# One DRAM record for each step of the RWKV recurrence, and exponents copied through DRAM

## The chip, the core and the metric

The kernel is one program on one NeuronCore of a Trainium2 chip. Its five engines have a queue each and run it in the order written: TensorE (PE in the profile, its weight loads PEld), VectorE (DVE), ScalarE (ACT), GpSimd (POOL) and SyncE (SP, which here only issues DMA transfers). The metric is the device time of one execution in microseconds.

## The reference

One layer of a hybrid block over a context of 256 tokens and 1024 latent tokens, width 1024. The normed and modulated input goes through one projection `h @ w_in` that feeds three groups; their outputs are joined and projected back; then a mixture of experts follows. The group that the change touches most is RWKV-7, four heads of 64, run forward and backward:

```python
def step(s, inp):
    r_t, w_t, k_t, v_t, a_t, b_t = inp
    sa = jnp.einsum('bhvk,bhk->bhv', s, a_t)
    s = s * w_t[:, :, None, :] + sa[..., None] * b_t[:, :, None, :] + v_t[..., None] * k_t[:, :, None, :]
    return s, jnp.einsum('bhvk,bhk->bhv', s, r_t)
```

The second group is a state space model (Mamba-2, chunks of 128), whose exponents are differences of a running sum: `decay_in = exp(where(causal, a_cs[..., :, None] - a_cs[..., None, :], -inf))`. The third is gated linear attention (GLA, chunks of 64), which carries a state of 32 by 64 a head from chunk to chunk.

## The kernel before, in words

RWKV is computed in chunks of 64 tokens, 20 of them for the 1280 tokens. Work on a chunk has three parts.

*Segments* (`rw_seg`, line 401). A segment is 256 tokens of one pair of heads (block b = 0 or 1); with five segments and two directions d a block has ten segment-directions. Each gives, per chunk: AR (decayed -kk and r), BK (b and k, decayed the other way), G (the 128x128 products of BK and AR under a mask: `psg`, line 463, and line 465), and BT, a transpose of BK (`ptb`, line 478). v is transposed as well (`ptv`, line 419). All this is stored to DRAM from SP: `vtD` (v), `mabD` (the half of G for the same head: MA in columns 0 to 63 and MB in 64 to 127), and `stepD` (AR, the other half of G, and BT, in 1536 columns for each chunk). That is 11 stores for a segment-direction. Tiles AR, BK, G have two buffers, BT one.

*Inverses* (`rw_inverse`, line 511). MA is read from `mabD` and a triangular inverse is built from it in 32x32 pieces (`px`); it goes to `sD`. There are three calls, the first 4 chunks of both blocks last (`i1`).

*Recurrence* (`rw_step`, line 599, 20 steps). `rw_loads` (line 576) reads the step's operands: `cd` from `stepD` (768 KB), half of `sm` from `sD`, from step 4 on the other half from `mabD` (MB, two loads), and `v` from `vtD` (two loads): six loads. Then a chain on TensorE, ScalarE and VectorE: pa from v and the state Z, copied to rh; pb from S and rh, copied to u; pz from v and u, added into the next Z. `py` is the output (latent chunks only).

Between these, TensorE does the big projection of the input (`psi`, lines 261 to 263): weights come in tiles of 512 KB (`wraw`, line 250, three buffers, loaded by SP too), are split into a high and a low part (whi, wlo), and multiply the 1280 tokens in pieces of 512 and 256 columns. Where the recurrence runs, the work of the other groups stands between its steps: GLA's states (`gla_states`, ptk and pkv), the exponents of the state space model (`ssd_dt`) and its states. `ssd_dt` puts the three bf16 parts of the running sums (`parts`, tile csp) into `difD`, from which `df` is read later; it takes 48 small stores (lines 1056 to 1058).

The order in each queue is set at build time by the framework's scheduler, from dependencies, buffers and its own estimates of durations. So a change of tiles and transfers can move instructions far from the lines that the diff touches.

Of the kernel before, what the change touches and what calls it, by code (L numbers as in the profile page):

```python
# [16 lines left out]
F = mybir.dt.float32  # L17
# [3 lines left out]
AF = mybir.ActivationFunctionType  # L21
# [9 lines left out]
TT = TC + TL  # L31
# [283 lines left out]
HS = [slice(0, 64), slice(64, 128)]  # L315
# [10 lines left out]
def rw_consts(g):  # L326
    nc, P = g.nc, g.ab
# [15 lines left out]

    g.stepD = g.dram.tile([128, 20, 1536], F, name="stepD")

    g.mabD = g.dram.tile([2, 128, 20, 2, 128], F, name="mabD")
    g.sD = g.dram.tile([2, 128, 20, 128], F, name="sD")
    g.vtD = g.dram.tile([20, 64, 512], F, name="vtD")
    g.bvD = g.dram.tile([2, 128, TL], F, name="bvD")
# [51 lines left out]
def rw_seg(g, b, s, r, k, v, wa, kk):  # L401

    nc = g.nc
    t0, n, pos = SEGS[s]
    T = lambda tag, bufs=2, w=256: g.tmp.tile([128, w], F, tag=tag, name=tag, bufs=bufs)
    ts = slice(t0, t0 + n)
    r, k, v, wa, kk = r[:, ts], k[:, ts], v[:, ts], wa[:, ts], kk[:, ts]
    nch = n // 64
    for d in range(2):
        p0, bd = pos[d], 2 * b + d  # L410
        pp = slice(p0, p0 + nch)
        if d:
            vd = T("sq")[:, 0:n]
            nc.scalar.activation(vd[:, ::-1], v, AF.Copy)
        else:
            vd = v
        pt = g.ps.tile([128, 4, 128], F, tag="tp", name="ptv")
        for i in range(n // 128):
            nc.tensor.transpose(pt[:, i, :], vd[:, 128 * i:128 * i + 128], g.ident)
        vt = T("vt", 2, 258)[:, 0:n].rearrange("p (i c) -> p i c", c=128)  # L420
        nc.scalar.activation(vt, pt[:, 0:n // 128], AF.Copy)
        nc.sync.dma_start(g.vtD[pp, :, 128 * bd:128 * bd + 128].rearrange("(i q) t c -> (q t) i c", q=2), vt)
        ps = g.ps.tile([128, 2, 256], F, tag="tp", name="psl")
# [35 lines left out]
        G = T("G", 2, 1024).rearrange("p (c h t) -> p c h t", h=2, t=128)[:, 0:nch]  # L459
# [6 lines left out]
        for h in range(2):  # L466
            o, u = HS[h], HS[1 - h]
            x0 = 384 * bd
            nc.sync.dma_start(g.mabD[b, o, pp, d], G[o, :, h, :])
            nc.sync.dma_start(g.stepD[o, pp, x0:x0 + 128], arf[o])  # L470
            nc.sync.dma_start(g.stepD[o, pp, x0 + 128:x0 + 256], G[u, :, h, :])
# [3 lines left out]
        for c0 in range(0, nch, 4):  # L475
            pt = g.ps.tile([128, 4, 128], F, tag="gm", name="ptb")
# [99 lines left out]
def rw_loads(g, p):  # L576

    nc, T = g.nc, g.rw
    cd = T.tile([128, 1536], F, tag="cd", name="cd", bufs=2)
    nc.sync.dma_start(cd, g.stepD[:, p])  # L580
    sm = T.tile([128, 2, 4, 64], F, tag="sm", name="sm", bufs=2)
    nc.sync.dma_start(sm[:, 0].rearrange("p (b q) t -> p b (q t)", b=2), g.sD[:, :, p].rearrange("b s t -> s b t"))
    if p >= 4:
        for b in range(2):
            nc.sync.dma_start(sm[:, 1, 2 * b:2 * b + 2], g.mabD[b, :, p, :, 64:128])
    v = T.tile([128, 4, 64], F, tag="v", name="v", bufs=3)
    for h in range(2):
        nc.sync.dma_start(v[HS[h]], g.vtD[p].rearrange("t (q h c) -> t q h c", q=4, h=2)[:, :, h, :])
    return cd.rearrange("p (q k t) -> p k q t", q=4, k=6), sm, v

# [8 lines left out]
def rw_step(g, p):  # L599
# [3 lines left out]
    at = lambda t: lambda q, h: t[h, q]  # L603
    cd, sm, v = rw_loads(g, p)
    a, r, ak, rk, bb, bk = (cd[:, k] for k in range(6))
    S, MB = sm[:, 0], sm[:, 1]
    ps = lambda tag, name: g.ps.tile([128, 4, 64], F, tag=tag, name=name)
# [43 lines left out]
def rw_finish(g):  # L651
    nc = g.nc
    for b in range(2):
        for t0 in (0, 512):
            ts = slice(t0, t0 + 512)
            x = g.rw.tile([128, 1536], F, tag="cd", name="fw", bufs=2)
            yc, bv, gt = (x[:, 512 * i:512 * i + 512] for i in range(3))
            sq = g.rw.tile([128, 512], F, tag="sm", name="fs", bufs=2)
            nc.sync.dma_start(bv, g.bvD[b, :, ts])
# [129 lines left out]
def gla_states(g):  # L789

    nc = g.nc
    W = g.gl
    glT = W.tile([16, TT], F, name="glT")
    for tl in range(10):
# [4 lines left out]
    g.gq = [W.tile([128, 3, TL], F, name=f"gq{d}") for d in range(2)]  # L799
    g.gS = W.tile([128, 2, 20, 64], F, name="gS")  # L800
    sc = 32 ** -0.5
# [10 lines left out]
    for d in range(2):  # L812
        nc.scalar.activation(la[:, d], la[:, d], AF.Ln, bias=g.epsc[:, 3:4])
        nc.gpsimd.tensor_sub(la[:, d], g.gq[d].rearrange("p i t -> p (i t)")[:, 0:TT], la[:, d])
    for d in range(2):
        rv = (lambda x: x[:, ::-1]) if d else (lambda x: x)
# [164 lines left out]
def ssd_dt(g):  # L981
# [64 lines left out]
    for i in range(3):  # L1046
        nc.vector.tensor_copy(parts[:, 0:2, i], cs)
        if i < 2:
            nc.vector.tensor_sub(cs, cs, parts[:, 0:2, i])
    nc.vector.tensor_scalar(parts[:, 2], parts[:, 0], -1.0, None, op0=OP.mult)  # L1050
    for d in range(2):
        for q in range(2):
            for h in range(4):
                src = parts[64 * d + 4 * q + h:64 * d + 64:8]
                o = 64 * q + 3 * h
                nc.sync.dma_start(g.difD[:, o + 12 * d:o + 12 * d + 3, h], src[:, 0])
                nc.sync.dma_start(g.difD[:, o + 24:o + 27, 4 + d], src[:, 2])
                nc.sync.dma_start(g.difD[:, o + 24:o + 27, 6 + d], src[:, 1])

# [807 lines left out]
```

## Time and profile before

| | us |
|---|---|
| median of 3 runs | 1532.99 |
| lowest, highest | 1532.07, 1540.90 |
| profiled execution | 1533.99 |
| its span | 1532.2 |
| TensorE busy | 1340.5 (87%) |
| VectorE busy | 785.2 (51%) |
| mean granted TensorE clock | 0.89 of full |

The stages follow one another: norm and first projections to about 120 us, segments of block 0 and 1 to about 411 us, convolution and inverses to about 556 us (both with projections between them), the recurrence to about 738 us, outputs of the state space model and GLA to about 905 us, then output projection and experts. A window row gives busy time of each engine, so the fullest engine of a stretch can be seen; a timeline row gives one run of like instructions with the wait ahead of it in brackets; the table of waits says what a tile's instruction waited for. An SP row is the time to issue a transfer, not to land it.

### The profile page before, as it was taken

The page shows a single profiled execution, that of the slowest core. Times are in us where ns is not written, and L with a number is a line of the kernel's source. Part 1 is how long each engine was busy: PE and PEld are TensorE (multiplying, and loading weights), DVE is VectorE, ACT ScalarE, POOL GpSimd, SP SyncE. Part 2 cuts the span into 40 slices and gives each one's busy share as a digit, 9 for nine tenths or more (in the row PEclk, how much of TensorE's full clock was granted, in tenths as well). Part 3 has the DMA queues.
Part 4 walks back from the last instruction along what each step waited for, and adds up shares of the span by engine and source line. Part 5 has one row for each costly group of instructions (what it writes and reads, how often), then busy time and mean ns, then how long its engine had stood idle before and what let it go on. Part 6 is the DMA issues. An engine that isn't in the chain of part 4 may idle for free. (4 is left out here: it accounts for less than half of the span.)

```text
span 1532.2 us, 28018 instructions
## 1 busy us (share of the span) xinstructions
PE 1340.5 (87%) x11077; PEld 1111.9 (73%) x11077; DVE 785.2 (51%) x1482; ACT 515.4 (34%) x1056; POOL 389.5 (25%) x432
## 2 busy tenths in 40 slices
PE   7897899999797776777889989993999999999984
PEld 3585677777676774666557767762999999999984
DVE  4849868889979854414564472227102212112532
ACT  5544334443363134422433352220212212212333
POOL 3312432343334111413453252112101111111112
PEclk9997899999899777889856589995999999999998
DMA  9454867677661467476544365425988868868984
GB/s 320 134 156 138 201 153 169 167 189 180 162 144 31 93 141 203 127 229 207 185 145 118 97 208 171 145 97 193 368 299 288 271 201 301 294 224 299 311 266 123
DMA packets 297253, 296.81 MB, mean 194 GB/s; under 512 B 114281, under 2 KB 214890, under 8 KB 297119
## 3 DMA queue, kind: packets, MB, share of 16 engines
q1 hardware_dynamic: 288095, 269.81, 57.7%
q0 software_dynamic: 7872, 20.97, 5.7%
q10 hardware_dynamic: 1152, 4.19, 0.7%
q8 instruction: 89, 1.46, 0.4%
q14 instruction: 45, 0.37, 0.1%
HBM read 221.44 MB, written 73.72 MB: 193 GB/s over the span
## 5 line engine op out<-in xcount | busy, mean ns | idle before, releaser
L1576 PE MATMUL p<-hT,w 128*128 128x144 f32 (+10 forms) x2048 | 263.2, 288 | 0.0
L1576 PEld LDWEIGHTS p<-hT,w 128*128 128x128 f32 x2048 | 257.6, 192 | 0.6
L262 PE MATMUL psi<-hlo,whi 128*128 128x512 f32 (+1 forms) x440 | 172.0, 391 | 5.0 <-DVE hlo L234 3.8
L261 PE MATMUL psi<-hhi,whi 128*128 128x512 f32 (+1 forms) x440 | 170.3, 389 | 0.0
L263 PE MATMUL psi<-hhi,wlo 128*128 128x512 f32 (+1 forms) x440 | 169.9, 387 | 0.3 <-POOL wlo L254 0.3
L1583 PE MATMUL p<-hid,w 128*128 128x144 f32 (+10 forms) x1024 | 136.6, 294 | 8.4 <-DVE hid L1578 7.2
L1583 PEld LDWEIGHTS p<-hid,w 128*128 128x128 f32 x1024 | 133.9, 199 | 9.0 <-DVE hid L1578 7.5
L1602 POOL DMA_INDIRECT acc<-yr,rows x27 | 41.4, 1532 | 323.0 <-DVE yr L1598 188.2
L1578 DVE TENSOR_TENSOR hid<-hid,p 128x144 f32<-128x144 f32 (+10 forms) x64 | 18.7, 294 | 170.0 <-PE p L1576 165.9
L262 PEld LDWEIGHTS psi<-hlo,whi 128*128 128x128 f32 x440 | 85.6, 195 | 26.0 <-DVE hlo L234 5.6
L263 PEld LDWEIGHTS psi<-hhi,wlo 128*128 128x128 f32 x440 | 85.4, 194 | 19.1 <-issue 3.4
L261 PEld LDWEIGHTS psi<-hhi,whi 128*128 128x128 f32 x440 | 85.8, 195 | 17.7 <-issue 2.1
L1598 DVE TENSOR_SCALAR yr<-pty,rows 128x512 f32<-128x512 f32 (+8 forms) x46 | 32.7, 741 | 112.4 <-PE pty L1592 105.2
L1584 ACT ACTIVATE yT<-p,mods 128x144 f32<-128x144 f32 (+10 forms) x128 | 43.0, 374 | 112.7 <-PE p L1583 112.5
L1577 ACT ACTIVATE hid<-p 128x144 f32<-128x144 f32 (+10 forms) x64 | 18.2, 284 | 168.8 <-PE p L1576 168.7
L739 DVE SCALAR_TENSOR_TENSOR co<-gr,pc,co 128x512 f32<-128x512 f32 x72 | 59.4, 849 | 6.5 <-ACT co L728 4.7
L190 DVE SCALAR_TENSOR_TENSOR aacc<-wada,csig,aacc 128x512 f32<-128x512 f32 x56 | 51.6, 921 | 15.6 <-DMA wada<-in_ada_w_dram 15.3
L262 PE MATMUL pso<-wol,mh 128*128 128x512 f32 x128 | 52.8, 412 | 3.3 <-DVE wol L1222 2.2
L261 PE MATMUL pso<-woh,mh 128*128 128x512 f32 x128 | 52.4, 412 | 1.0 <-DVE go L1265 1.0
L263 PE MATMUL pso<-woh,ml 128*128 128x512 f32 x128 | 52.6, 411 | 0.0
L463 PE MATMUL psg<-AR,BK 64*128 64x128 f32 x320 | 46.6, 304 | 4.0 <-DVE BK L456 1.6
L463 PEld LDWEIGHTS psg<-AR,BK 64*128 64x128 f32 x320 | 39.5, 204 | 13.4 <-issue 4.0
(540 smaller groups left out, 2668.3 us busy)
## 6 DMA issues: line engine op xcount, KB each, us to landing
w<-in_moe_w_dram SPq DMA_DIRECT2D x47, 2048.0 KB
wada<-in_ada_w_dram SPq DMA_DIRECT2D x32, 512.0 KB
cd<-stepD SPq DMA_DIRECT2D x20, 768.0 KB
wraw<-in_w_in_dram SPq DMA_DIRECT2D x24, 512.0 KB
aw<-in_ada_w_dram SPq DMA_DIRECT2D x10, 512.0 KB
stepD<-AR SPq DMA_DIRECT2D x40, 128.0 KB
mabD<-G SPq DMA_DIRECT2D x40, 128.0 KB
stepD<-G SPq DMA_DIRECT2D x40, 128.0 KB
```

What stands on the lines that cost most here:

```text
L190: nc.vector.scalar_tensor_tensor(acc, w[:, k % 2], g.sg[:, k, 0:1], acc, op0=OP.mult, op1=OP.add)
L261: nc.tensor.matmul(ps, whi(k), xhi(k), start=k == 0, stop=False)
L262: nc.tensor.matmul(ps, whi(k), xlo(k), start=False, stop=False)
L263: nc.tensor.matmul(ps, wlo(k), xhi(k), start=False, stop=k == 7)
L463: nc.tensor.matmul(pg[h][:, c, :], bkf[HS[h], c], arf[HS[h], c], start=True, stop=True)
L739: nc.vector.scalar_tensor_tensor(o, src(dy, dx), w(3 * dy + dx), o, op0=OP.mult, op1=OP.add)
L1576: nc.tensor.matmul(p[:, 0:n], w[:, k, fs], hT[:, k, s0:s0 + n], start=k == 0, stop=k == 7)
L1578: nc.vector.tensor_mul(hid[:, f, 0:n], hid[:, f, 0:n], p3[:, 0:n])
L1583: nc.tensor.matmul(p[:, 0:n], w2[:, f, 128 * k:128 * k + 128], hid[:, f, 0:n], start=f == 0, stop=f == 3)
L1584: nc.scalar.activation(yT[:, k, 0:n], p[:, 0:n], AF.Copy, scale=g.mods[:, 40 + k, 0:1])
L1598: nc.vector.tensor_scalar(yr[0:m, h], pf, wt[0:m, b:b + 1], None, op0=OP.mult)
L1602: nc.gpsimd.indirect_dma_start(out=g.acc, out_offset=bass.IndirectOffsetOnAxis(ap=rows[0:m, 0, b:b + 1], axis=0), in_=yr[0:m, :], in_offse ...
```

## The change

- `stepD` grows from 1536 to 2048 columns: MB (columns 64 to 127 of G's half) and v go into it. `vtD` is dropped and `mabD` holds MA alone. In a segment, each of the two stores of G to `mabD` becomes two stores of half the width, and v is transposed in 64x64 blocks, so that it lies by head as the record wants it. A segment-direction has 13 stores instead of 11; 80 of G's stores are 64 KB with 256-byte pieces.
- A step of the recurrence loads `rec` (1024 KB) and `S` (128 KB), each with three buffers, where it had six loads and two buffers (three for v). Steps 0 to 3 now load MB as well, which they don't use.
- `difD` is filled from a DRAM copy of the parts: one store to `partsD`, then 24 copies from DRAM to DRAM.
- `glT` shares a buffer with `gS`, and `rw_finish` uses the tile `rec`.

```diff
--- before.py
+++ after.py
@@ -341,11 +341,10 @@
     g.PC = P.tile([128, 4, 20], F, name="PC")
 
 
-    g.stepD = g.dram.tile([128, 20, 1536], F, name="stepD")
-
-    g.mabD = g.dram.tile([2, 128, 20, 2, 128], F, name="mabD")
+    g.stepD = g.dram.tile([128, 20, 2048], F, name="stepD")
+
+    g.mabD = g.dram.tile([2, 128, 20, 2, 64], F, name="mabD")
     g.sD = g.dram.tile([2, 128, 20, 128], F, name="sD")
-    g.vtD = g.dram.tile([20, 64, 512], F, name="vtD")
     g.bvD = g.dram.tile([2, 128, TL], F, name="bvD")
     g.gtD = g.dram.tile([2, 128, TL], F, name="gtD")
 
@@ -414,12 +413,13 @@
             nc.scalar.activation(vd[:, ::-1], v, AF.Copy)
         else:
             vd = v
-        pt = g.ps.tile([128, 4, 128], F, tag="tp", name="ptv")
-        for i in range(n // 128):
-            nc.tensor.transpose(pt[:, i, :], vd[:, 128 * i:128 * i + 128], g.ident)
-        vt = T("vt", 2, 258)[:, 0:n].rearrange("p (i c) -> p i c", c=128)
-        nc.scalar.activation(vt, pt[:, 0:n // 128], AF.Copy)
-        nc.sync.dma_start(g.vtD[pp, :, 128 * bd:128 * bd + 128].rearrange("(i q) t c -> (q t) i c", q=2), vt)
+        pt = g.ps.tile([128, 4, 64], F, tag="tp", name="ptv")
+        for i in range(nch):
+            for h in HS:
+                nc.tensor.matmul(pt[h, i, :], vd[h, 64 * i:64 * i + 64], g.ident[h, h], start=True, stop=True)
+        vt = T("vt", 2, 258)[:, 0:n].rearrange("p (i c) -> p i c", c=64)
+        nc.scalar.activation(vt, pt, AF.Copy)
+        nc.sync.dma_start(g.stepD[:, pp, 1792 + 64 * bd:1856 + 64 * bd], vt)
         ps = g.ps.tile([128, 2, 256], F, tag="tp", name="psl")
         sa = T("sa", 2, 512).rearrange("p (q t) -> p q t", q=2)
         for q in range(2):
@@ -466,7 +466,8 @@
         for h in range(2):
             o, u = HS[h], HS[1 - h]
             x0 = 384 * bd
-            nc.sync.dma_start(g.mabD[b, o, pp, d], G[o, :, h, :])
+            nc.sync.dma_start(g.mabD[b, o, pp, d], G[o, :, h, 0:64])
+            nc.sync.dma_start(g.stepD[o, pp, 1536 + 64 * bd:1600 + 64 * bd], G[o, :, h, 64:128])
             nc.sync.dma_start(g.stepD[o, pp, x0:x0 + 128], arf[o])
             nc.sync.dma_start(g.stepD[o, pp, x0 + 128:x0 + 256], G[u, :, h, :])
 
@@ -576,17 +577,12 @@
 def rw_loads(g, p):
 
     nc, T = g.nc, g.rw
-    cd = T.tile([128, 1536], F, tag="cd", name="cd", bufs=2)
-    nc.sync.dma_start(cd, g.stepD[:, p])
-    sm = T.tile([128, 2, 4, 64], F, tag="sm", name="sm", bufs=2)
-    nc.sync.dma_start(sm[:, 0].rearrange("p (b q) t -> p b (q t)", b=2), g.sD[:, :, p].rearrange("b s t -> s b t"))
-    if p >= 4:
-        for b in range(2):
-            nc.sync.dma_start(sm[:, 1, 2 * b:2 * b + 2], g.mabD[b, :, p, :, 64:128])
-    v = T.tile([128, 4, 64], F, tag="v", name="v", bufs=3)
-    for h in range(2):
-        nc.sync.dma_start(v[HS[h]], g.vtD[p].rearrange("t (q h c) -> t q h c", q=4, h=2)[:, :, h, :])
-    return cd.rearrange("p (q k t) -> p k q t", q=4, k=6), sm, v
+    rec = T.tile([128, 2048], F, tag="rec", name="rec", bufs=3)
+    nc.sync.dma_start(rec, g.stepD[:, p])
+    S = T.tile([128, 4, 64], F, tag="S", name="S", bufs=3)
+    nc.sync.dma_start(S.rearrange("p (b q) t -> p b (q t)", b=2), g.sD[:, :, p].rearrange("b s t -> s b t"))
+    MB, v = (rec[:, o:o + 256].rearrange("p (q t) -> p q t", q=4) for o in (1536, 1792))
+    return rec[:, 0:1536].rearrange("p (q k t) -> p k q t", q=4, k=6), S, MB, v
 
 
 def heads(g, out, lhs, rhs, start, stop):
@@ -601,9 +597,8 @@
 
     nc, T = g.nc, g.rw
     at = lambda t: lambda q, h: t[h, q]
-    cd, sm, v = rw_loads(g, p)
+    cd, S, MB, v = rw_loads(g, p)
     a, r, ak, rk, bb, bk = (cd[:, k] for k in range(6))
-    S, MB = sm[:, 0], sm[:, 1]
     ps = lambda tag, name: g.ps.tile([128, 4, 64], F, tag=tag, name=name)
     pa, Z = ps("ch", "pa"), None
     heads(g, pa, ak, at(v), True, p == 0)
@@ -653,9 +648,8 @@
     for b in range(2):
         for t0 in (0, 512):
             ts = slice(t0, t0 + 512)
-            x = g.rw.tile([128, 1536], F, tag="cd", name="fw", bufs=2)
-            yc, bv, gt = (x[:, 512 * i:512 * i + 512] for i in range(3))
-            sq = g.rw.tile([128, 512], F, tag="sm", name="fs", bufs=2)
+            x = g.rw.tile([128, 2048], F, tag="rec", name="fw", bufs=3)
+            yc, bv, gt, sq = (x[:, 512 * i:512 * i + 512] for i in range(4))
             nc.sync.dma_start(bv, g.bvD[b, :, ts])
             nc.sync.dma_start(gt, g.gtD[b, :, ts])
             pm = g.ps.tile([128, 512], F, tag="ch", name="pm")
@@ -790,14 +784,13 @@
 
     nc = g.nc
     W = g.gl
-    glT = W.tile([16, TT], F, name="glT")
+    glT = W.tile([16, TT], F, tag="gS", name="glT", bufs=1)
     for tl in range(10):
         pt = g.ps.tile([128, 512], F, tag="gl", name="ptg")
         nc.tensor.transpose(pt[0:16, 0:128], g.vg[:, tl, 256:272], g.ident)
         nc.scalar.activation(glT[:, 128 * tl:128 * tl + 128], pt[0:16, 0:128], AF.Copy)
     T = lambda tag, bufs=1: W.tile([128, 512], F, tag=tag, name=tag, bufs=bufs)
     g.gq = [W.tile([128, 3, TL], F, name=f"gq{d}") for d in range(2)]
-    g.gS = W.tile([128, 2, 20, 64], F, name="gS")
     sc = 32 ** -0.5
 
     la = W.tile([128, 2, TT], F, tag="la", name="la")
@@ -812,6 +805,7 @@
     for d in range(2):
         nc.scalar.activation(la[:, d], la[:, d], AF.Ln, bias=g.epsc[:, 3:4])
         nc.gpsimd.tensor_sub(la[:, d], g.gq[d].rearrange("p i t -> p (i t)")[:, 0:TT], la[:, d])
+    g.gS = W.tile([128, 2, 20, 64], F, tag="gS", name="gS", bufs=1)
     for d in range(2):
         rv = (lambda x: x[:, ::-1]) if d else (lambda x: x)
         end, mid = (0, 31) if d else (63, 32)
@@ -1048,14 +1042,17 @@
         if i < 2:
             nc.vector.tensor_sub(cs, cs, parts[:, 0:2, i])
     nc.vector.tensor_scalar(parts[:, 2], parts[:, 0], -1.0, None, op0=OP.mult)
+
+    pD = g.dram.tile([3, 128, 3, 128], BF, name="partsD")
+    nc.sync.dma_start(pD.rearrange("k p i t -> p k (i t)"), parts.rearrange("p k i t -> p k (i t)"))
     for d in range(2):
         for q in range(2):
             for h in range(4):
-                src = parts[64 * d + 4 * q + h:64 * d + 64:8]
-                o = 64 * q + 3 * h
-                nc.sync.dma_start(g.difD[:, o + 12 * d:o + 12 * d + 3, h], src[:, 0])
-                nc.sync.dma_start(g.difD[:, o + 24:o + 27, 4 + d], src[:, 2])
-                nc.sync.dma_start(g.difD[:, o + 24:o + 27, 6 + d], src[:, 1])
+                o = 64 * q + 12 * d + 3 * h
+                nc.sync.dma_start(g.difD[:, o:o + 3, h], pD[0, 64 * d + 4 * q + h:64 * d + 64:8])
+            for to, k in ((4, 2), (6, 1)):
+                nc.sync.dma_start(g.difD[:, 64 * q + 24:64 * q + 36, to + d],
+                                  pD[k, 64 * d:64 * d + 64].rearrange("(c q h) i t -> q c (h i) t", q=2, h=4)[q])
 
 
 def ssd_states(g):
```

Three places in the order. First TensorE in block 0. Before, near the start of the block (psl and ptv are other products of a segment, wa_495 the tile of its gate inputs, psa a product of the conditioning):

```order
L463 MATMUL psg<-AR,BK 128x128 x4
L426 MATMUL psl<-wa,wa_495 128x256
L463 MATMUL psg<-AR,BK 128x128 x4
L419 MATMUL ptv<-ident,sq 128x128 x2
L193 MATMUL psa<-onesm,aacc 128x1 x4
L261 MATMUL psi<-hhi,whi 128x512
L262 MATMUL psi<-hlo,whi 128x512
L261 MATMUL psi<-hhi,whi 128x512
L262 MATMUL psi<-hlo,whi 128x512
L426 MATMUL psl<-wa,wa_495 128x256
L478 MATMUL ptb<-ident,BK 128x128 x4
L263 MATMUL psi<-hhi,wlo 128x512
```

and after the change, at the end of block 0 (pbo is the block's bonus term):

```order
L463 MATMUL psg<-AR,BK 128x128 x8
L495 MATMUL pbo<-rk,blk_91 128x256
L479 MATMUL ptb<-ident,BK 128x128 x4
L495 MATMUL pbo<-rk,blk_91 128x256 x2
L463 MATMUL psg<-AR,BK 128x128 x8
L495 MATMUL pbo<-rk,blk_91 128x256
L479 MATMUL ptb<-ident,BK 128x128 x4
L261 MATMUL psi<-hhi,whi 128x512
L262 MATMUL psi<-hlo,whi 128x512
L261 MATMUL psi<-hhi,whi 128x512
L262 MATMUL psi<-hlo,whi 128x512
L263 MATMUL psi<-hhi,wlo 128x512
```

Before, 284 psi stand between the first and the last psg of block 0, and 91 between block 0 and block 1; now none and 336. Behind the last psg of block 1, 336 were left and are now 383.

Second, SP in block 0. Before, in its first stores:

```order
L469 DMA mabD<-G 64x4x128
L471 DMA stepD<-G 64x4x128
L469 DMA mabD<-G 64x4x128
L471 DMA stepD<-G 64x4x128
L250 DMA wraw<-in_w_in_dram 128x8x128
L484 DMA stepD<-BT 64x4x64 x4
L469 DMA mabD<-G 64x4x128
```

and now, at its end:

```order
L472 DMA stepD<-G 64x4x128
L469 DMA mabD<-G 64x4x64
L470 DMA stepD<-G 64x4x64
L471 DMA stepD<-AR 64x4x128
L472 DMA stepD<-G 64x4x128
L485 DMA stepD<-BT 64x4x64 x4
L498 DMA bvD<-bv 128x256 x2
L250 DMA wraw<-in_w_in_dram 128x8x128
L186 DMA wada<-in_ada_w_dram 128x2x512 x2
L498 DMA bvD<-bv 128x256 x2
L530 DMA Dm<-mabD 32x32x32 x4
L186 DMA wada<-in_ada_w_dram 128x2x512 x2
```

The load of weights that stood behind the first six stores of G and AR stands now behind the last BT store of the block.

Third, SP at the start of the recurrence. Before (sD<-t are the last stores of the inverse, vgD and xsD tiles of the other groups):

```order
L580 DMA cd<-stepD 128x1536
L582 DMA sm<-sD 128x2x128
L588 DMA v<-vtD 64x4x64 x2
L580 DMA cd<-stepD 128x1536
L582 DMA sm<-sD 128x2x128
L588 DMA v<-vtD 64x4x64 x4
L743 DMA xsD<-co 128x512 x2
L582 DMA sm<-sD 128x2x128
L588 DMA v<-vtD 64x4x64 x2
L573 DMA sD<-t_4881 32x32x32 x2
L580 DMA cd<-stepD 128x1536
```

and now:

```order
L764 DMA vgD<-vgo 128x280 x3
L737 DMA xsD<-co 128x256
L574 DMA sD<-t_5040 32x32x32 x2
L581 DMA rec<-stepD 128x2048
L583 DMA S<-sD 128x2x128
L581 DMA rec<-stepD 128x2048
L583 DMA S<-sD 128x2x128
L581 DMA rec<-stepD 128x2048
L583 DMA S<-sD 128x2x128 x2
```

The first record's load has moved behind the last two stores of the inverse. And in the middle of the recurrence, the stores to difD, before:

```order
L1058 DMA difD<-csp 8x3x128
L588 DMA v<-vtD 64x4x64 x2
L1056 DMA difD<-csp 8x3x128
L580 DMA cd<-stepD 128x1536
L1057 DMA difD<-csp 8x3x128
L1058 DMA difD<-csp 8x3x128
L1056 DMA difD<-csp 8x3x128
L1057 DMA difD<-csp 8x3x128
L582 DMA sm<-sD 128x2x128
L585 DMA sm<-mabD 128x2x64 x2
L1058 DMA difD<-csp 8x3x128
L1056 DMA difD<-csp 8x3x128
```

and now:

```order
L581 DMA rec<-stepD 128x2048
L583 DMA S<-sD 128x2x128
L1047 DMA partsD<-csp 128x3x384
L581 DMA rec<-stepD 128x2048
L1052 DMA difD<-partsD 8x3x128 x4
L1054 DMA difD<-partsD 8x12x128 x2
L1052 DMA difD<-partsD 8x3x128 x4
L1054 DMA difD<-partsD 8x12x128
L583 DMA S<-sD 128x2x128
L1054 DMA difD<-partsD 8x12x128
L1052 DMA difD<-partsD 8x3x128 x4
L1054 DMA difD<-partsD 8x12x128 x2
```

The 48 stores stood between the loads of seven steps; 24 copies stand now between the loads of three. On TensorE, the px of the last inverse now have psi between them and not step 0, and 7 ptk with 56 pkv stand in the recurrence instead of 13 with 100; the other 6 tiles stand behind it.

## Rows read from the trace of the kernel before

**Rows 1.** Windows: length; PE, PEld, DVE, ACT, POOL busy us; PEclk, DMA share, GB/s.

```profile
140.00:160.00 20.00, 14.38 (x59) 11.70 (x60) 19.83 (x34) 6.87 (x17) 8.04 (x9) 0.50 0.69 172
160.00:180.00 20.00, 20.00 (x102) 15.59 (x102) 16.11 (x24) 8.82 (x20) 6.45 (x6) 0.90 0.92 254
460.00:560.00 100.00, 75.54 (x534) 67.77 (x532) 85.05 (x170) 26.46 (x44) 25.22 (x27) 0.86 0.36 75
640.00:680.00 40.00, 27.78 (x612) 24.19 (x607) 6.29 (x16) 8.09 (x24) 3.74 (x5) 0.79 0.67 200
```

**Rows 2.** Timeline of PE, segments and projections: start us, us, engine, line, op, [idle].

```profile
140.89 3.10 PE L463 MATMUL psg<-AR,BK 64*128 64x128 f32 x16 [1.60 <-DVE BK L456]
147.90 2.24 PE L463 MATMUL psg<-AR,BK 64*128 64x128 f32 x10
157.74 0.77 PE L261 MATMUL psi<-hhi,whi 128*128 128x512 f32 x1
...
258.87 1.16 PE L463 MATMUL psg<-AR,BK 64*128 64x128 f32 x8
...
544.78 0.40 PE L261 MATMUL psi<-hhi,whi 128*128 128x512 f32 x1
...
552.95 0.39 PE L263 MATMUL psi<-hhi,wlo 128*128 128x512 f32 x1
```

**Rows 3.** Timeline of SP's queue in block 0.

```profile
146.34 0.58 SPq L469 DMA_DIRECT2D mabD<-G  x1
149.01 0.90 SPq L250 DMA_DIRECT2D wraw<-in_w_in_dram  x1
150.00 2.63 SPq L484 DMA_DIRECT2D stepD<-BT  x4
154.88 1.24 SPq L470 DMA_DIRECT2D stepD<-AR  x2
159.60 1.09 SPq L422 DMA_DIRECT2D vtD<-vt  x2
```

**Rows 4.** Timeline of PE, then one row of SP, around the last inverse.

```profile
556.81 0.28 PE L563 MATMUL px<-t,t 32*32 32x32 f32 x2 [3.47 <-DMA t<-mabD]
560.89 1.88 PE L563 MATMUL px<-t,t 32*32 32x32 f32 x62 [3.80 <-DMA t<-mabD]
563.63 0.44 PE L596 MATMUL pa<-v,cd 64*64 64x64 f32 x2 [0.86 <-ACT t L565]
573.30 1.06 PE L596 MATMUL pa<-v,cd 64*64 64x64 f32 x16
...
573.12 0.94 SPq L573 DMA_DIRECT2D sD<-t  x2
```

**Rows 5.** Waits of PE from 573 to 739: total us, times, longest.

```profile
PE pa L596 <- DMA cd<-stepD: 13.9, 5, 5.0
PE pa L596 <- issue: 4.7, 2, 4.1
```

**Rows 6.** Timeline of PE and SP in the recurrence's steps.

```profile
647.34 0.57 SPq L1058 DMA_DIRECT2D difD<-csp  x1
652.47 0.38 SPq L580 DMA_DIRECT2D cd<-stepD  x1
...
656.90 1.12 PE L596 MATMUL pa<-v,cd 64*64 64x64 f32 x16 [5.00 <-DMA cd<-stepD]
...
675.57 0.63 PE L596 MATMUL pa<-v,cd 64*64 64x64 f32 x16
677.07 0.38 PE L859 MATMUL pkv<-vg,ke 64*32 64x64 f32 x16
680.89 0.68 PE L596 MATMUL pa<-v,cd 64*64 64x64 f32 x16 [0.15 <-PE pz L596]
...
738.08 0.63 PE L596 MATMUL py<-sm,u 64*64 64x64 f32 x16
```

**Rows 7.** Groups of PE from 738 to 906: busy us, mean ns | idle.

```profile
L849 PE MATMUL ptk<-ident,kend 128*128 128x128 f32 x7 | 2.6, 367 | 0.0
```

## Prediction

> **What bounds the kernel now.** I read the windows first. Three stretches matter, because the diff touches what runs in them. While the first block of RWKV segments runs, TensorE is busy for 14.38 of 20 us between 140 and 160 us and for all 20 between 160 and 180 us; VectorE is below it from there on [rows 1]. Projection matmuls (psi) fill TensorE between the segments' own products. Between 460 and 560 us it is the other way round: VectorE 85 of 100 us, TensorE 75.5 [rows 1]. Between 640 and 680 us, in the recurrence, VectorE has only 6.29 of 40 us of work and TensorE 27.78 at a mean clock of 0.79 [rows 1]: something else is waited for.
>
> The timeline of TensorE then gives the pace of a segment. The first products (psg) of block 0 stand at 140.89 us, the next at 147.90, the last at 258.87; the first psi after a pause stands at 157.74, and psi of 512 columns at full speed start 0.234 us apart (36 rows from 544.78 to 552.95) [rows 2]. SyncE's issues show why that psi stands at 157.74: its weights were issued at 149.01, in the queue behind segment stores of about 0.6 us each [rows 3]. From issue to first use: 8.7 us.
>
> The end of the inverse shows TensorE waiting 3.47 and 3.80 us for tiles from DRAM while step 0 of the recurrence already starts at 563.63; by 573.30 it begins step 1 [rows 4]. In the recurrence the table of waits has 13.9 us of pa for the record's load and 4.7 us of pa for "issue", its queue [rows 5]. A load issued at 652.47 is used at 656.90, after 4.4 us; further on a whole step takes 5.3 us (675.57 to 680.89) [rows 6].
>
> **The change, part by part.** (1) *Block 0, the largest term.* Each segment-direction issues 13 stores where it issued 11. With 0.58 us for a piece of G, 1.24 for two AR, 2.63 for four BT and half of 1.09 for v [rows 3], that is 6 x 0.58 + 1.24 + 2.63 + 0.55 = 7.9 us of SyncE. By the order listing, no psi stands between the first and the last psg of block 0 any more (284 stood there), and the next psi's weights are issued behind the last BT store. So TensorE's filler is gone for the whole block. Pace: 7.0 us between the first two psg [rows 2] is the low bound, 7.9 is SyncE's own, and I take 8.0; the high bound is 9.5, where two G buffers also wait for six stores of each to land. The last psg then stands at 141 + 9 x 8.0 = 213; the last products, stores and BT take another 10; weights to first psi 8.7: TensorE's stream starts again at 232 (221 to 245). The order puts 336 psi between the blocks in place of 91. Of the 336, 284 make up the deficit; at 0.234 us for 512 columns [rows 2] and half for 256 they are 61 us, so TensorE reaches at 293 what it had at 260: 33 us late. 47 psi (11 us) stand behind the last psg of block 1 now that stood ahead of it, so 22 us stay (11 to 35), if the DVE-bound stretch behind takes those 11 us in its idle 24 of TensorE [rows 1]. **+22 us.**
>
> The 120 more small matmuls for v (160 of 64x64 instead of 40) fall in this same stretch, where TensorE now has nothing else: nothing. If that cover went, 0.63 us for 16 products of 64x64 [rows 6] gives 120 x 0.04 = 5 us.
>
> (2) *Last inverse.* In the order listing its 64-matmul stages now have psi between them, where step 0 stood. That covers the two waits of 3.47 and 3.80 [rows 4]: **-7 us** (0 to -8).
>
> (3) *Start of the recurrence.* The first rec load now stands behind the last sD stores, issued at 573.12 and taking 0.94 [rows 4]; before, the loads stood ahead. The record grows from 768 to 1024 KB; 4.4 us [rows 6] scaled by bytes is 5.9. Step 0 begins at 574 + 6 = 580, where before step 1 began at 573.3: 6.7 us and one step of 5.3 later, **+12 us**.
>
> The Trainium skill ("DMA: Bandwidth & Descriptors", section on the anatomy of one DMA) gives about 2 us fixed plus bytes at 436 GB/s, measured there on GpSimd's path; that estimate is 4.4 us for 1 MiB, and 3.8 for 768 KB where the trace shows 4.4. By it term (3) would be 10.5 and the total 1.5 us less. The trace's figure is used.
>
> (4) *Steps.* With three buffers, two loads in place of six and the 48 difD stores (32 us of SyncE between the loads at about 0.6 each [rows 6]) replaced by one store and 24 copies in one place, the waits of 13.9 and 4.7 go [rows 5]: -18.6. After each of them pa runs at the lower clock: 1.12 us for 16 products at 656.90, 0.63 at 675.57 [rows 6]; 27.78 us of TensorE at 0.79 would be 22 at full clock, 6 us [rows 1]. **-25 us** (-12 to -34). Next late is then TensorE itself: 5.3 us a step against 1.15 MB, which at the 200 GB/s of [rows 1] are 5.8 us when loads and other traffic share and less when they run ahead.
>
> (5) *Exponents (difD).* partsD and the copies add a round trip through DRAM. The first copy waits on SyncE until partsD has landed, and the first df load, a few rows on, until the copies have; behind both stand loads of rec and S for the next steps. Two records loaded ahead cover that, 10.6 us of steps at 5.3, and df itself is read behind the recurrence. If the cover is gone, it costs two landings of about 4.4 us, the nearest row being the 768 KB load [rows 6]: 9 us at most. I take nothing.
>
> (6) *Tail.* 6 GLA tiles (44 pkv, 6 ptk in the listing) move from the recurrence to behind it. With 0.367 us for ptk and 0.38 for the 16 pkv of a tile [rows 6, 7], a tile is 0.75 us: **+4 us** (0 to +8 at half clock). The glT/gS sharing and rw_finish's tile only change which buffer is reused; both have their data long before, nothing.
>
> Sum: +22 - 7 + 12 - 25 + 4 = +6 on the profiled execution's 1534.0 us, which is 1.0 above the median 1533.0: **1539 us** rounded.
>
> **Rivals.**
> *The stores of block 0 hold longer (slower).* Place: SyncE in block 0, G's two buffers. For it: 13 issues in order, one queue, and the weights' load behind all. Against: before, 147.90 came 7.0 us after 140.89. From a pace of 9.0 us on, the lag at the recurrence is 31 and the total +15; at 10.5 us it is 44 and the total +28: 1549 to 1562. Chance 0.22.
> *The record saves nothing (slower).* If the recurrence's loads are bound by bytes, not by issues, the -25 shrinks to -8 (the queue's 4.7 and little clock): +23, 1557. For it: more bytes in the first four steps. Against: in 640 to 680 us the DMA engines are busy for only 0.67 of the time [rows 1]. Chance 0.07.
> *Small pieces (slower).* A seg-direction's stores in 256-byte pieces grow (v, both halves of G). The Trainium skill ("DMA: Bandwidth & Descriptors", Specifications) says that below 512 bytes the engines read, modify and write. No row shows the price of it alone. From bytes: 1152 KB a segment-direction, of which 640 KB in such pieces; counted twice, they are 1.8 MB, at the 254 GB/s of [rows 1] 7.2 us, under the 8.0 taken. Only at three times (9.8 us) would it decide: +22, 1556. Chance 0.03.
> *The lag is caught up (faster).* From 460 to 560 us TensorE is idle for 24 us [rows 1], and VectorE gets projections' results in one go after block 0, so its later work can run ahead. If the lag at the recurrence is 0 to 8 in place of 22, the sum is -16 to -8; with the recurrence at its low end, -25: 1509 to 1526, 1514 in the middle. For it: VectorE's slack in block 0. Against: the listing leaves the inverse in block 1, and both streams are in order. Chance 0.28.
>
> **How the numbers follow.** The forecast, terms (1) and (4) nearly cancelling, has chance 0.40. By its own terms' bounds it spans 1520 to 1556; most of it lies within 1% (15 us, about what a measurement here tells from no change). Faster by over 1% takes the third of a total of -15 and below: 0.28 from the last rival. Slower: 0.22 + 0.07 + 0.03 = 0.32. The range must leave out no more than 2 in 10: 1508 to 1565 leaves the outer ends of the first and last rival.
>
> **What would show it.** Block 0: a stretch of some 90 us with TensorE under 10 of 20 us busy, and the first psi near 232. Recurrence: first pa some 6 us after sD's stores, no pa wait on rec above 1 us after step 4, pa to pa 5 to 6 us between steps 5 and 19. The tail: po of GLA later by some 4 us relative to the last py. The forecast is wrong if psi starts again before 215 or after 250, if the stretch from sD's stores to the last step is not 5 to 22 us shorter (165.0 us before, 573.1 to 738.1 [rows 4, 6]), or if the lag of the blocks is no longer there when the inverse ends.

## The result, and the profile after

The change is slower: 1583.7 us median against 1534.3, ratio 1.030 with a 95% interval of 1.027 to 1.034. The profiled execution took 1578.8 us, its span 1576.6, 44.4 us more than before. The forecast was 1539 and the range 1508 to 1565, so it was wrong.

Where the 44.4 us went, from the ends of the last rows of each stage in the two timelines:

| | before | after | difference |
|---|---|---|---|
| first psg of block 1 | 288.6 | 322.7 | +34.1 |
| end of the last px (inverses) | 572.5 | 611.7 | +39.2 |
| last px to last py (recurrence) | 166.2 | 145.8 | -20.4 |
| last py to last pso (outputs, projection) | 290.1 | 311.6 | +21.5 |
| last pso to the end (experts) | 503.4 | 507.5 | +4.1 |

The first row lies inside the second, and the other four make up the 44.4. Each is from one trace. Over the traces of the sixteen kernels below, the last stage, which no edit touches, took from 498.2 to 509.3 us, so differences of a few us in a single stage mean little, the +4.1 among them.

First TensorE in block 0 after the change (start us, us, engine, line, op, idle in brackets), which answers to [rows 2]:

```profile
140.84 3.09 PE L463 MATMUL psg<-AR,BK 64*128 64x128 f32 x16 [0.65 <-DVE BK L456]
149.22 2.24 PE L463 MATMUL psg<-AR,BK 64*128 64x128 f32 x10
...
218.13 3.07 PE L463 MATMUL psg<-AR,BK 64*128 64x128 f32 x16
222.43 1.12 PE L479 MATMUL ptb<-ident,BK 128*128 128x128 f32 x4
238.56 0.79 PE L261 MATMUL psi<-hhi,whi 128*128 128x512 f32 x1 [15.02 <-ACT whi L252]
...
322.67 1.16 PE L463 MATMUL psg<-AR,BK 64*128 64x128 f32 x16
```

The first two psg stand 8.4 us apart where it was 7.0. Then nothing but segment products until 222.43, and 15.02 us of full stop before the first psi at 238.56. The windows (length; PE, PEld, DVE, ACT, POOL busy; PEclk, DMA share, GB/s) answer to [rows 1]:

```profile
140.00:160.00 20.00, 15.36 (x88) 12.62 (x89) 19.67 (x34) 5.81 (x16) 8.30 (x9) 0.50 0.59 128
160.00:220.00 60.00, 49.94 (x244) 38.96 (x243) 44.24 (x82) 18.52 (x48) 22.95 (x26) 0.50 0.73 129
220.00:260.00 40.00, 24.90 (x111) 20.04 (x110) 12.69 (x19) 7.02 (x10) 3.42 (x2) 0.70 0.90 214
260.00:300.00 40.00, 40.00 (x190) 31.87 (x190) 15.98 (x16) 15.21 (x22) 5.51 (x8) 1.00 0.22 64
```

From 160 to 220 us TensorE is granted half its clock throughout, which is the 1.2 GHz level; before, it had 0.90 already from 160 to 180 us. It is busy for 49.94 of 60 us there, so the sign in the forecast, under 10 of 20 us, did not come: at half clock the segments' own products fill most of the time. The last segment-directions of the block on SP's queue answer to [rows 3]:

```profile
220.64 2.56 SPq L485 DMA_DIRECT2D stepD<-BT  x4
223.25 0.60 SPq L422 DMA_DIRECT2D stepD<-vt  x1
223.95 0.57 SPq L469 DMA_DIRECT2D mabD<-G  x1
224.57 0.61 SPq L470 DMA_DIRECT2D stepD<-G  x1
225.28 0.57 SPq L471 DMA_DIRECT2D stepD<-AR  x1
225.90 0.61 SPq L472 DMA_DIRECT2D stepD<-G  x1
226.61 0.57 SPq L469 DMA_DIRECT2D mabD<-G  x1
227.23 0.62 SPq L470 DMA_DIRECT2D stepD<-G  x1
227.90 0.61 SPq L471 DMA_DIRECT2D stepD<-AR  x1
228.56 0.61 SPq L472 DMA_DIRECT2D stepD<-G  x1
229.27 2.56 SPq L485 DMA_DIRECT2D stepD<-BT  x4
231.88 1.08 SPq L498 DMA_DIRECT2D bvD<-bv  x2
233.00 0.45 SPq L250 DMA_DIRECT2D wraw<-in_w_in_dram  x1
```

From one group of BT to the next, 220.64 to 229.27, are 8.63 us without a stop: SyncE issues 13 stores back to back at 0.57 to 0.64 us each, with 0.05 to 0.10 between two rows. Behind the last stands the load of weights, at 233.00.

From the last psg of block 1 to the last px, before (two waits of TensorE and the window) and then in the change (pst is another piece of the input projection):

```profile
PE px L563 <- DMA t<-mabD: 16.1, 5, 6.6
PE pst L261 <- ACT gr L719: 8.3, 1, 8.3
400.61:572.50 171.89, 134.49 (x1295) 118.46 (x1296) 135.36 (x247) 64.30 (x108) 47.39 (x57) 0.83 0.50 113
```

```profile
PE pst L261 <- ACT gr L713: 11.2, 1, 11.2
PE pst L261 <- DVE vgo L763: 9.3, 1, 9.3
PE px L564 <- DMA t<-mabD: 8.8, 3, 5.8
435.74:611.70 175.96, 138.44 (x1278) 119.46 (x1277) 128.16 (x234) 59.12 (x99) 41.82 (x54) 0.85 0.43 95
```

The lag, 35.1 us at the last psg of block 1 (435.7 against 400.6), grows by 4.1 here. TensorE's idle time is 37.4 us before and 37.5 after: the waits of px fell by 7.3 us, and those of pst grew by more.

The end of the inverses, the first pa of steps 0 and 1 and the last py answer to [rows 4, 6]:

```profile
610.51 1.19 PE L569 MATMUL px<-t,t 32*32 32x32 f32 x62
614.99 0.40 PE L263 MATMUL psi<-hhi,wlo 128*128 128x512 f32 x1
620.38 1.12 PE L592 MATMUL pa<-rec 64*64 64x64 f32 x16 [4.99 <-DMA rec<-stepD]
...
624.58 1.06 PE L592 MATMUL pa<-rec 64*64 64x64 f32 x16
...
756.86 0.68 PE L592 MATMUL py<-rec,u 64*64 64x64 f32 x16
```

Before, step 0 ran inside the last inverse, and step 1 began at 573.30, 0.8 us behind the last px; now it begins 12.9 us behind it. From there to the last py are 132.9 us, where it was 165.4. Two waits for the record are left, 11.2 us, the last over at 639.7 us, where [rows 5] had 18.6 for the record and its queue (total us, times, longest):

```profile
PE py L592 <- DMA rec<-stepD: 6.2, 1, 6.2
PE pa L592 <- DMA rec<-stepD: 5.0, 1, 5.0
```

Last, the stretch from the last py to the last pso, in the change and then before it:

```profile
757.50:1069.10 311.60, 281.48 (x2023) 197.01 (x2022) 149.01 (x254) 113.89 (x188) 104.91 (x91) 0.77 0.42 136
```

```profile
738.70:1028.80 290.10, 271.98 (x1930) 192.51 (x1928) 131.07 (x231) 102.87 (x168) 98.20 (x85) 0.81 0.45 145
```

The change has 9.5 us more of PE busy there, at a clock of 0.77 for 0.81, and 12.0 us more of idle.

### The profile page after: what moved, and what is told of

It reads as the page before. It is cut to its first block, busy times and chain, and to the rows that moved or that the text cites. A ratio compares the mean times of both kernels' runs of the same rounds, so it can differ in the third digit from the quotient of the medians.

```text
span 1576.6 us, 28466 instructions
## 1 busy us (share of the span) xinstructions
PE 1363.4 (86%) x11357; PEld 1129.4 (72%) x11357; DVE 788.3 (50%) x1482; ACT 519.5 (33%) x1058; POOL 386.7 (25%) x432
## 5 line engine op out<-in xcount | busy, mean ns | idle before, releaser
L1580 PEld LDWEIGHTS p<-hid,w 128*128 128x128 f32 x1024 | 135.2, 200 | 11.2 <-DVE hid L1575 8.4
L190 DVE SCALAR_TENSOR_TENSOR aacc<-wada,csig,aacc 128x512 f32<-128x512 f32 x56 | 47.9, 856 | 22.5 <-DMA wada<-in_ada_w_dram 22.0
L463 PE MATMUL psg<-AR,BK 64*128 64x128 f32 x320 | 58.0, 360 | 1.1 <-DVE BK L456 0.6
L463 PEld LDWEIGHTS psg<-AR,BK 64*128 64x128 f32 x320 | 50.8, 256 | 8.9 <-issue 4.1
```

The source lines that it names most:

```text
L190: nc.vector.scalar_tensor_tensor(acc, w[:, k % 2], g.sg[:, k, 0:1], acc, op0=OP.mult, op1=OP.add)
L463: nc.tensor.matmul(pg[h][:, c, :], bkf[HS[h], c], arf[HS[h], c], start=True, stop=True)
L1580: nc.tensor.matmul(p[:, 0:n], w2[:, f, 128 * k:128 * k + 128], hid[:, f, 0:n], start=f == 0, stop=f == 3)
```

## The experiments

Each time is the median; the ratio is to the kernel before run beside it, which took 1540.0 to 1543.2 us in the rounds of the experiments. "px", "recurrence" and "tail" are the end of the last px, last px to last py, and last py to last pso in the profiled execution.

| run | median us | ratio (95%) | px | recurrence | tail |
|---|---|---|---|---|---|
| before | 1534.3 | | 572.5 | 166.2 | 290.1 |
| the change | 1583.7 | 1.030 (1.027 to 1.034) | 611.7 | 145.8 | 311.6 |
| split_store_alone | 1607.2 | 1.045 (1.041 to 1.049) | 612.4 | 181.8 | 304.0 |
| split_second_half_gpsimd | 1533.0 | 0.998 (0.995 to 1.002) | 578.1 | 163.3 | 291.5 |
| mb_on_gpsimd | 1531.6 | 0.994 (0.990 to 0.997) | 582.2 | 154.0 | 288.9 |
| g_stored_whole | 1545.5 | 1.003 (0.999 to 1.006) | 575.8 | 155.7 | 303.3 |
| weights_on_gpsimd | 1533.0 | 0.993 (0.991 to 0.996) | 587.8 | 154.4 | 285.6 |
| third_buffer_alone | 1524.3 | 0.991 (0.988 to 0.994) | 580.0 | 152.6 | 283.0 |
| record_two_buffers | 1547.2 | 1.005 (1.002 to 1.008) | 580.2 | 168.3 | 290.0 |
| dif_copies_alone | 1517.4 | 0.984 (0.979 to 0.990) | 578.0 | 156.2 | 280.7 |
| buffers_and_copies | 1514.9 | 0.983 (0.978 to 0.987) | 578.0 | 144.7 | 284.9 |
| copies_and_shared_tile | 1519.2 | 0.986 (0.982 to 0.989) | 576.8 | 160.6 | 280.8 |
| copies_mab_on_gpsimd | 1525.8 | 0.990 (0.986 to 0.993) | 569.2 | 161.5 | 292.2 |
| record_old_stores | 1534.8 | 0.995 (0.992 to 0.998) | 584.0 | 160.8 | 284.1 |
| gla_all_behind | 1582.9 | 1.029 (1.021 to 1.038) | 569.0 | 92.9 | 406.4 |
| gla_tiles_delayed | 1536.9 | 0.998 (0.995 to 1.002) | 585.0 | 151.1 | 293.3 |

### What empties block 0

```diff
-nc.sync.dma_start(g.mabD[b, o, pp, d], G[o, :, h, :])
+for z in (0, 64):
+    nc.sync.dma_start(g.mabD[b, o, pp, d][:, :, z:z + 64], G[o, :, h, z:z + 64])
```

> The kernel before, with one edit: each store of G's half to mabD is issued as two stores of half the width (40 more issues on SyncE, the same bytes, nothing else). Its order listing has no psi in block 0, as the change has. Theory A (the added issues on SyncE empty block 0 of projections, and that lag stays): the first psg of block 1 30 to 36 us later than before, last px of the inverses 30 to 42 us later, time 1560 to 1575. Theory B (the lag is caught up before the recurrence ends, and what costs time is the later part: GLA moved behind the recurrence): time 1530 to 1545. Theory C (the 256-byte pieces cost transfer time, not issue time): the last psg of block 0 later than 230 us, and DMA share in block 0 near 1.

It came to 1.045, more than the change itself. TensorE's rows at the end of block 0, and the wait of pa in its recurrence:

```profile
219.47 3.06 PE L463 MATMUL psg<-AR,BK 64*128 64x128 f32 x16
...
239.95 0.80 PE L261 MATMUL psi<-hhi,whi 128*128 128x512 f32 x1 [15.07 <-ACT whi L252]
```

```profile
PE pa L597 <- DMA cd<-stepD: 28.3, 9, 5.9
```

The pause is the change's (psi again at 239.95, px 39.9 us late). What theory A had too low is the rest: the recurrence is 15.6 us longer than before, as the waits of pa on cd doubled to 28.3 us, and the tail 13.9. Theory B and its number are out.

The counter-test has the same pieces, half of the stores on GpSimd's queue:

```diff
-    nc.sync.dma_start(g.mabD[b, o, pp, d][:, :, z:z + 64], ...
+    (nc.gpsimd if z else nc.sync).dma_start(g.mabD[b, o, pp, d][:, :, z:z + 64], ...
```

> The kernel before with G's store split in two as in the split alone (1607), the second half issued from GpSimd's queue: the same pieces and as many issues, 40 of them elsewhere. Its order listing has 284 psi in block 0, as before. If SyncE's queue is the cause (theory A): 1528 to 1545, first psg of block 1 within 6 us of before. If the pieces are (theory C): last psg of block 0 after 268, over 1550.

No difference from before; the first psg of block 1 stands at 292.6. So the pieces are not the cause (theory C), SyncE's queue is. The same in the change:

```diff
-nc.sync.dma_start(g.stepD[o, pp, 1536 + 64 * bd:1600 + 64 * bd], G[o, :, h, 64:128])
+nc.gpsimd.dma_start(g.stepD[o, pp, 1536 + 64 * bd:1600 + 64 * bd], G[o, :, h, 64:128])
```

> The change, with one edit: the 40 stores of MB into the record are issued from GpSimd's queue in place of SyncE's. Its order listing has 264 psi in block 0 again. Theory A: block 0's lag goes (first psg of block 1 within 8 us of before), and the recurrence keeps its gain of some 20 us: 1525 to 1550. Theory B: 1570 or more, since the tail is as in the change. Theory C: as B, since the pieces are the same.

From 1.030 to 0.994, 3.6% are back. The tail is back too, at 288.9 us, with 16 GLA tiles in the recurrence instead of 7: the one edit to the stores changed that order as well. On SyncE the weights' load stands among the first segment-directions again:

```profile
148.05 1.30 SPq L469 DMA_DIRECT2D mabD<-G  x1
149.40 0.62 SPq L472 DMA_DIRECT2D stepD<-G  x1
150.11 0.56 SPq L250 DMA_DIRECT2D wraw<-in_w_in_dram  x1
```

GpSimd takes 642 ns to issue one of the stores it got (minimum, median, maximum ns; first and last start):

```profile
L470 POOL DMA_DIRECT2D stepD<-G x40: 631/642/845, 147.0 to 415.3; - x40
```

Two more ways to the same end: G stored whole with MB loaded from mabD, and the weights' loads issued from GpSimd.

```diff
-nc.sync.dma_start(g.mabD[b, o, pp, d], G[o, :, h, 0:64])
-nc.sync.dma_start(g.stepD[o, pp, 1536 + 64 * bd:1600 + 64 * bd], G[o, :, h, 64:128])
+nc.sync.dma_start(g.mabD[b, o, pp, d], G[o, :, h, :])
...
+            nc.sync.dma_start(MB[:, 2 * b:2 * b + 2], g.mabD[b, :, p, :, 64:128])
```

> The change, with one part undone: G's half is stored in one piece to mabD as before, and MB is loaded from there by two loads a step into three buffers; v stays in the record (1792 columns). Its order listing has 254 psi in block 0. Theory A: first psg of block 1 within 10 us of before, 1530 to 1560; two more loads a step cost the recurrence 0 to 10 us. Theory B: 1570 or more.

```diff
-nc.sync.dma_start(raw[:, :, o:o + b - a], ...
+nc.gpsimd.dma_start(raw[:, :, o:o + b - a], ...
```

> The change, with the weight loads of the input projection issued from GpSimd's queue; all 13 stores of a segment-direction stay on SyncE. Its order listing has 264 psi in block 0. If the weights' place behind the stores empties block 0 (theory A): last psg of block 0 at 250 to 268, first psg of block 1 within 10 us of before, 1520 to 1550. If the load of issues on SyncE by itself makes the block longer: last psg of block 0 after 270, 1555 and more.

Both bring the projections back into block 0, whose last psg ends at 255.2 and 260.8 us. The second keeps all 13 stores on SyncE, so the load of issues alone does not stretch the block: it is that the weights are behind them. Its first psg of block 1 stands at 298.3, 9.7 us later than before, and its last px 15.3, which no run explains. In all runs the pause on TensorE is there exactly where the order listing has no psi in block 0, so what the added stores did, they did through the scheduler's order as well as in the queue; no run has the one without the other.

### What shortens the recurrence

Three buffers alone, with glT in gS's buffer as in the change:

```diff
-cd = T.tile([128, 1536], F, tag="cd", name="cd", bufs=2)
+cd = T.tile([128, 1536], F, tag="cd", name="cd", bufs=3)
-sm = T.tile([128, 2, 4, 64], F, tag="sm", name="sm", bufs=2)
+sm = T.tile([128, 2, 4, 64], F, tag="sm", name="sm", bufs=3)
```

> The kernel before, with three buffers for cd and sm, and glT in gS's buffer, which gives the room; six loads a step and 48 difD stores as before. If the recurrence's gain comes from the buffers: pa's waits on cd fall from 13.9 us to under 4, stretch from sD's stores to the last py 10 to 20 us shorter, 1515 to 1528. If it comes from fewer issues on SyncE: waits stay over 10 us, 1530 to 1537.

No wait of pa on cd is left and the recurrence is 13.6 us shorter: the first outcome. The other way round, the record with two buffers (on mb_on_gpsimd's stores):

```diff
-rec = T.tile([128, 2048], F, tag="rec", name="rec", bufs=3)
+rec = T.tile([128, 2048], F, tag="rec", name="rec", bufs=2)
-S = T.tile([128, 4, 64], F, tag="S", name="S", bufs=3)
+S = T.tile([128, 4, 64], F, tag="S", name="S", bufs=2)
```

> The change with MB's stores on GpSimd's queue (1531.6 with three buffers), and two buffers for rec and S in place of three. If the gain in the recurrence is the third buffer's: waits of pa and py on rec of 10 us and more, 1540 to 1552. If it is the fewer loads': 1526 to 1536.

Its waits, and then those of the same kernel with three buffers:

```profile
PE pa L592 <- DMA rec<-stepD: 19.7, 15, 3.4
```

```profile
PE py L592 <- DMA rec<-stepD: 3.1, 1, 3.1
```

So with the record the third buffer is worth 14.3 us in the recurrence, and fewer loads without it bring nothing. The exponents' copies alone, with the lines of the change:

```diff
+    nc.sync.dma_start(pD.rearrange("k p i t -> p k (i t)"), parts.rearrange("p k i t -> p k (i t)"))
...
-                nc.sync.dma_start(g.difD[:, o + 12 * d:o + 12 * d + 3, h], src[:, 0])
+                nc.sync.dma_start(g.difD[:, o:o + 3, h], pD[0, 64 * d + 4 * q + h:64 * d + 64:8])
...
```

> The kernel before, with the exponents' part of the change alone: partsD and 24 copies in place of 48 stores; two buffers and six loads a step. If the 48 issues between the loads made pa wait: waits on cd and issue under 8 us, 1515 to 1526. If the buffers did (the third buffer alone left no wait of pa on cd): waits stay, 1528 to 1538. If the round trip through DRAM costs: over 1540.

They give 1.6% by themselves, the time of the first of the three outcomes:

```profile
PE pa L596 <- issue: 9.0, 4, 5.7
PE pa L596 <- DMA cd<-stepD: 3.5, 4, 1.6
PE pa L596 <- DMA v<-vtD: 3.5, 1, 3.5
```

cd's 13.9 us of [rows 5] are 3.5, so the 48 stores between the loads did delay them. But the wait for the queue grew from 4.7 to 9.0, so cd and issue together are 12.5 us and not under 8; the recurrence is 10.0 us shorter, the tail 9.4. The two edits together, and the record (mb_on_gpsimd) with the 48 old stores:

> The kernel before with two parts of the change: three buffers for cd and sm (with glT in gS's buffer), and the exponents by partsD and 24 copies. Six loads a step and the segments' stores as before. If the two gains add (third buffer 0.991, copies 0.984): 1500 to 1512. If both remove the same waits: 1515 to 1524. Its order listing has 13 GLA tiles in the recurrence where the copies alone have 16; by what moved tiles cost (about 2.4 us a tile over the runs so far) it may lose 7 us of that.

> The change with MB's stores on GpSimd's queue (1531.6) and the exponents stored as before by 48 stores. If with three buffers the 48 issues cost nothing: 1526 to 1536. If they cost as much as in the kernel before (16 to 24 us): 1545 to 1556.

0.983 against 0.984 and 0.991 singly: by time they don't add beyond the interval, though the recurrence is the shortest of the six-load kernels that keep the other groups' work in it. This is the fastest version found, not to be told from the copies alone by its time, and it has no record. Under the record with three buffers the copies change nothing that can be told (0.994 and 0.995). Two variants of the copies brought nothing more, glT's sharing without a third buffer, and the stores to mabD issued by `nc.gpsimd` in place of `nc.sync`:

> The kernel before with the copies and with glT in gS's buffer, two buffers and six loads. Its order listing in the recurrence is that of the copies alone (16 tiles). If the shared tile costs nothing: as the copies alone, 1512 to 1523. If it makes GLA wait: over 1526.

> The kernel before with the copies, and the 40 stores to mabD issued from GpSimd's queue in place of SyncE's; two buffers, six loads. If SyncE's issues still hold block 0 back there: first psg of block 1 at 275 to 285, 1500 to 1513. If not: 1512 to 1524.

The second missed its number: the first psg of block 1 stayed at 288.6, and the tail was 11.5 us longer than with the copies alone.

### What lengthens the tail

> The kernel before with three buffers for cd and sm, without the room that glT's sharing gives: its order listing has no GLA tile and no state of the state space model in the recurrence (before: 13 tiles, 19 pss), all of it stands behind. Upstream and loads are as in the run with the third buffer alone, 1524.3. If moved work costs its matmuls alone (0.75 us a tile as the prediction had it): the recurrence ends 30 to 45 us earlier and the stretch from the last py to the last pyd grows by as much, total 1515 to 1535. If a moved tile costs some 2 to 3 us more than in the recurrence (17 us for 6 tiles in the change): the stretch grows by 35 us more than the recurrence gains, 1550 to 1575.

```profile
569.00:661.90 92.90, 78.66 (x2274) 74.01 (x2272) 11.99 (x37) 19.34 (x56) 11.20 (x18) 0.93 0.86 246
661.90:1068.30 406.40, 326.29 (x2244) 212.81 (x2244) 184.54 (x340) 140.28 (x248) 129.57 (x110) 0.72 0.39 123
```

The 20 steps alone take 92.9 us. This is the kernel of third_buffer_alone with glT in a buffer of its own (`glT = W.tile([16, TT], F, name="glT")`). The tail is 123 us longer than there and the recurrence 60 shorter, so the second outcome, and worse than its number. It moves all of the two groups' preparation, not tiles alone. The next run was meant to move tiles alone, on mb_on_gpsimd; `g.mark` is written from the output of the last step, and ten tiles have to wait for it:

```diff
+        if p == 19 and d == 1:
+            nc.gpsimd.tensor_copy(g.mark, dst[:, 0, 0:1])
...
+            if d or t0 == 768:
+                nc.gpsimd.tensor_copy(k[:, 0:1], g.mark)
             nc.sync.dma_start(k, g.sp["k"][:, t0:t1])
```

> The change with MB's stores on GpSimd's queue (1531.6, 16 GLA tiles in the recurrence), with one dependency more: the k loads of GLA's second direction and of the first direction's last chunk wait for step 19. By the order listing 6 tiles stand in the recurrence (the change: 7), block 0 and the inverses as in the run without it. If tiles behind the recurrence are what makes the change's tail longer: last py to last pso 302 to 315 us (289 without), last px to last py 140 to 150 (154 without), total 1536 to 1556. If the tail of the change is longer for another reason: last py to last pso 285 to 295, total 1524 to 1534.

The tail grew from 288.9 to 293.3 us, not to 302 or more; the median is 5 us up, within the two intervals. First with the tiles delayed, then without:

```profile
736.10:1029.40 293.30, 257.02 (x1978) 184.01 (x1976) 132.26 (x242) 103.17 (x173) 89.47 (x82) 0.80 0.41 133
```

```profile
736.20:1025.10 288.90, 269.86 (x1886) 191.56 (x1885) 132.68 (x226) 100.52 (x163) 99.01 (x85) 0.81 0.45 143
```

It did not move tiles alone. Ten tiles left the recurrence, and the states of the state space model (pss) took their place. With the tiles delayed, then without (minimum, median, maximum ns; first and last start):

```profile
L1096 PE MATMUL pss<-xs,B x72: 379/379/690, 618.3 to 721.8; 128*64 128x256 f32 x72
```

```profile
L1091 PE MATMUL pss<-xs,B x72: 379/430/688, 616.7 to 753.1; 128*64 128x256 f32 x72
```

With the delay all pss stand ahead of the last py at 736.1; without it some 30 stand behind. So the 4.4 us of the tail, and the 2.9 that the recurrence gave back, are ten tiles in one direction against these states in the other, and the price of a tile cannot be read from them. TensorE's busy time in the tail fell by 12.8 us, and its idle time rose from 19.0 to 36.3.

My reading of the earlier runs, in which long tails (303 to 312 us) and 7 tiles in the recurrence went together, is thus neither shown nor refuted. What the sixteen traces show is a correlation: TensorE's idle time in the tail is 12.7 to 23.5 us where 4 to 7 of the 20 ptk stand in it, 24.0 to 36.3 where 12 to 14 do (12 in the change, 6 before), and 80.1 with all 20. These orders differ in more than that.

## Why the prediction was wrong

The sum missed by 38.4 us: +24.2 up to the end of the inverses, -7.4 in the recurrence, +17.5 in the tail, +4.1 behind it, where nothing was forecast.

**Block 0 (term 1): right mechanism, mis-sized, and its second half wrong.** TensorE's filler went and psi waited for the last store, as worked out. The pace was 8.6 us, not 8.0, because I summed the issues without the pauses between them, 0.7 us a segment-direction; psi came back at 238.6, not 232. That is 6.6 us. The step that failed is the next: "22 us stay", with the 11 us of psi left for later to be taken up in TensorE's idle time behind block 1, and -7 for the inverse (term 2). The lag was 35.1 us when block 1's last psg ended, 13 more than 22; the 6.6 are half of that, and I cannot place all of the rest. In the stretch behind, where -7 was forecast, the lag grew by 4.1 to 39.2. The two waits of the last inverse did go, 7.3 us down to 0.9, but pst waited 11.8 us longer in all in the same stretch. So idle time was not used up (37.4 us before, 37.5 after), and TensorE's added work, 4.0 us busy, came on top. Terms 1 and 2 gave +15; measured +39.2.

**Recurrence (terms 3, 4, 5): +12 - 25 gave -13, measured -20.4.** Term 3 was right: step 1 begins 12.9 us behind the last px instead of 0.8, +12.1. From there to the last py it is 32.5 us shorter, where term 4 had 25; how much of this is the work that left the recurrence no run separates. The first record took 5.0 us from issue to use (615.4 to 620.4), where 5.9 was taken. The waits went as forecast but for one of py, 6.2 us; but the fewer loads of the record, which I named beside the buffers, were not what did it: the third buffer alone removes them, and the copies alone most of those on cd. The round trip through DRAM (term 5) costs nothing that shows.

**Tail (term 6): +4, measured +21.5 to the last pso.** The step that failed is to price a moved tile by its own products on TensorE, 0.75 us. TensorE was busy for 9.5 us more, at a lower clock, and idle for 12.0 more, of which the term had nothing. Whether the tiles themselves bring the idle time, or the order that the scheduler made anew, stays open: the run that was to tell moved other work the other way.

**Rivals.** None came as written. The nearest is "the stores of block 0 hold longer", but its condition, a pace of 9.0, was not met; at 8.6 its own working gives a lag of 27 us, not 39. "Small pieces" fell to the split with half of it on GpSimd. "The lag is caught up" fell: it grew. "The record saves nothing" fell too, since the recurrence is shorter; but the record is not needed for it: buffers and copies without it are at 0.983, with it and the stores moved to GpSimd at 0.994.

**Signs.** Of the three signs by which the forecast was to be known as wrong, none came: psi started again between 215 and 250, the stretch from sD's stores to the last step (612.4 to 756.9) is 20.5 us shorter, and the lag was still there. They did not bound the size of the lag, and none of the three looked at the length of the tail.

## What to carry to other kernels

Where one queue issues both stores and the next stage's weights, count its issues against the pace of the stage: two more stores for each 11 cost 3.6% here (1.030 against 0.994) and 4.5% in the kernel before, and from another queue they cost nothing (0.998). When an order listing shows a filler gone, price the whole lag to the end of the program; take recovery later only where a row shows idle time on both engines that it needs. Take a change of several parts one part at a time: here one part (0.984) and another (0.991) were gains, hidden behind a third.

## What the runs showed of the hardware

From 160 to 220 us TensorE was busy for 49.9 of 60 us and still granted 0.50 of its clock; before, from 140 to 160 us, 14.38 of 20 us busy went with 0.50 too [rows 1]. After psi began at 238.56, the window from 260 us on has 1.00.

A store of half the bytes, in as many pieces, took SyncE as long to issue. The store of G to mabD before (128 KB) and then in the change (64 KB):

```profile
L469 SPq DMA_DIRECT2D mabD<-G x40: 574/578/1497, 146.3 to 408.1; - x40
```

```profile
L469 SPq DMA_DIRECT2D mabD<-G x40: 574/575/1754, 147.0 to 443.1; - x40
```

Issuing a store of 64 KB takes GpSimd 642 ns, about as long as SyncE (0.57 to 0.62 us in the rows above).
